# Gathered table rows of a PEER layer: groups of 16 u rows and 16 v rows turned into single u and v rows, the v rows 22 behind

## Chip, core and metric

The kernel runs on one core of a Trainium2 chip. The metric is the device time of one execution in microseconds (us). TensorE (PE in the profile), VectorE (DVE), ScalarE (ACT), GpSimd (POOL) and SyncE (SP) each work through an instruction stream of their own, in order. SP starts most of the DMA transfers, POOL starts the gathers.

## What is computed

One layer of a streaming encoder: a convolution and a differential-attention head group, then a PEER layer, each with a residual and a layer norm. There are 544 tokens of width 1024: 512 of a prompt and 32 of running streams. The change lies in the PEER layer. For every token and each of 8 heads it picks 16 of 16384 rows of a table `u_tab` by product keys (two times 128 half scores, the best 16 of each, the best 16 of their sums), and then computes:

```python
a = jnp.einsum('td,thkd->thk', tb, u_tab[e]).astype(jnp.float32)
a = jax.nn.gelu(a, approximate=False) * g
return jnp.einsum('thk,thkd->td', a.astype(tb.dtype), v_tab[e])
```

`e` holds the 128 (8 heads of 16) row numbers of a token, and `g` their softmax weights.

## The kernel before

**Dense part.** For the first 384 tokens (three tiles of 128, `TA = 3`) the kernel multiplies with the whole tables. `u_part(j)`, called for j = 0 to 127, takes one block of 128 u rows: `split` loads it (`raw`, 512 KB, line 898, on SP's queue), ACT makes a rounded copy `hi` (L900), DVE the rest `lo = raw - hi` (L902), and PE runs 24 matmuls of 128x384 into one PSUM tile `pat` (L911): 8 with `hi`, 8 with `lo`, 8 with `hi` again (against the low half of the tokens). ACT puts the Gelu of `pat` into `ge` (L917). `v_part` and `v_mm` do the same with 128 blocks of v rows, 18 matmuls of 128x512 per block (L994).

**Gathered part.** The last 160 tokens do not go through the dense part. They stand in two tiles: one of 128 tokens, and one of 32 tokens in 4 copies, each copy with 32 of the 128 row numbers. So there are 128 + 32 = 160 *columns*, and for each column one gather of a u row and one of a v row: an indirect DMA on POOL (L847) that fetches 128 rows of 4 KB, one for each partition, into a buffer `rowg`, of which there are four. For a u row, DVE multiplies it with the tokens and sums up (L858, the *dot*, into one column of `aB`). For a v row, DVE adds it, times a weight of each partition, to the sum `accB` (L869, the *add*; the first is L867). The weights of 16 columns are the Gelu of 16 columns of `aB` (L861, ACT) times `GW` (L862, DVE). The generator `b_gather` emits this, one gather and its dot or add at each step: 320 steps in all, in groups of 16 u rows, Gelu, 16 v rows.

**What sets the order.** `gathers(rate)` takes some steps of the generator; `slot()` calls it after each `u_part` and each v block, and `query()` after each of its key blocks `hp` from the third on. `slot()` also emits pieces of the *background*, the choice of rows for the dense tokens (`level2`: top-16 searches, L661 to L666, and arithmetic, L721 to L773, on DVE) and their one-hot matrices (`onehots`: L810 to L817 on DVE, L826 on PE). Each gather is *paced*: it gets a dependence on a matmul, `ANCHOR[-1 - LAG]` with `LAG = 2`; the first matmul of each `u_part` is put on the list `ANCHOR`, so a gather that is emitted behind a `u_part` waits for the first matmul of the `u_part` two calls earlier. Behind all this stands a scheduler, which reorders the instructions of every engine by its own model of their times before the program is built; so the order in the source is only its input.

Of the kernel before, what the change touches and what calls it, by code (L numbers as in the profile page):

```python
# [8 lines left out]
F32 = mybir.dt.float32  # L9
F32R = mybir.dt.float32r  # L10
F16 = mybir.dt.float16
I32 = mybir.dt.int32
U32 = mybir.dt.uint32
AF = mybir.ActivationFunctionType
OP = mybir.AluOpType
# [4 lines left out]
D = 1024  # L20
# [7 lines left out]
TA = NA // 128  # L28
# [32 lines left out]
EXTRA = 8  # L61
RUN = 4
LAST = 4
CN = (3, -1)
CB = 4
CZ = 2
# [10 lines left out]
def build(tc, I, O):  # L77
# [3 lines left out]
    V, S, G, PE, SY = nc.vector, nc.scalar, nc.gpsimd, nc.tensor, nc.sync  # L81
# [165 lines left out]
    for c in range(4):  # L247
# [5 lines left out]
        for d0, h, s0, s1 in ((30, 0, 0, HT), (30 + HT, 1, 0, np2), (572, 1, np2, HT)):  # L253
            V.scalar_tensor_tensor(U[:, c, d0:d0 + s1 - s0], p0[:, h, s0:s1], bzc[:, c:c + 1], sg[:, h, s0:s1],
                                   op0=OP.add, op1=OP.mult)
# [26 lines left out]
    def conv(n):  # L282
        for _ in range(n):
            next(taps, None)
# [18 lines left out]
    for m in range(2):  # L303
        V.scalar_tensor_tensor(lj, lamv[:, 2 * m], 1.0, lamv[:, 2 * m + 1], op0=OP.mult, op1=OP.mult,
                               accum_out=lsum[:, m:m + 1])
# [123 lines left out]
    for h in range(4):  # L429
        qk = [None, None]  # L430
        for kind in (1, 0):
            n = 8 + 4 * kind + h
# [18 lines left out]
        qh, kh = qk  # L451
        if (h, -1) == CN:
            conv(124)
# [3 lines left out]
        for i in ((0, 1, 2, 3) if h < 3 else (3, 0, 1, 2)):  # L457
# [17 lines left out]
            conv(CB)  # L475
            if (h, i) == CN:
                conv(124)
# [45 lines left out]
    tk = pool(ctx, "tk", 1)  # L523
    idxB = [tk.tile([128, 128], I32, name="idx0"), tk.tile([128, 32], I32, name="idx1")]
    GWB = [tk.tile([128, 128 if i < 4 else 32], F32, name=f"GW{i}") for i in (3, 4)]
    aB = [tk.tile([128, 128], F32, name="aB0"), tk.tile([128, 32], F32, name="aB1")]
    VT, IT, IJ, GW = {}, {}, {}, {}
# [20 lines left out]
    for s in range(2):  # L548
        t = op_.tile([128, D], F32, tag="row", name="bg", bufs=4) if s == 0 else xhB[0]
# [123 lines left out]
    def run(g):  # L673
        for _ in g:
            pass
# [156 lines left out]
    accB = [gap.tile([128, D], F32, name=f"accB{s}") for s in range(2)]  # L832
    gp = pool(ctx, "gp", 1, side="right")
# [5 lines left out]
    h2B = xhB  # L839
# [5 lines left out]
    def gather(tab, idx):  # L845
        t = gp.tile([128, D], F32, tag="rowg", name="rowg", bufs=ROWB)
        g = G.indirect_dma_start(out=t, out_offset=None, in_=tab, in_offset=bass.IndirectOffsetOnAxis(ap=idx, axis=0))  # L847
        if len(ANCHOR) > LAG:
            tc.add_manual_dep(g.ins, ANCHOR[-1 - LAG].ins.name, DEP, reason="paced by the dense tiles")
        return t  # L850

    def b_gather():
        for s, n in ((0, 128), (1, 32)):
            for c0 in range(0, n, 16):
                for q in range(c0, c0 + 16):
                    t = gather(I["u_ji"], idxB[s][:, q:q + 1])
                    jk = gp.tile([128, D], F16, tag="jkg", name="jkg", bufs=1)
                    V.scalar_tensor_tensor(jk, t, 1.0, h2B[s], op0=OP.mult, op1=OP.mult, accum_out=aB[s][:, q:q + 1])  # L858
                    yield
                w = tk.tile([128, 16], F32, tag="wB", name="wB", bufs=2)  # L860
                S.activation(w, aB[s][:, c0:c0 + 16], AF.Gelu)  # L861
                V.tensor_mul(w, w, GW[TA + s][:, c0:c0 + 16])  # L862
                for q in range(c0, c0 + 16):
                    t = gather(I["vd"], idxB[s][:, q:q + 1])
                    ac = accB[s]
                    if q == 0:
                        V.tensor_scalar(ac, t, w[:, 0:1], None, op0=OP.mult)  # L867
                    else:
                        V.scalar_tensor_tensor(ac, t, w[:, q - c0:q - c0 + 1], ac, op0=OP.mult, op1=OP.add)  # L869
                    yield  # L870

    state = {"A": 0, "gdone": 0, "budget": 0.0, "gq": 0.0, "slots": 2 * NK}

    def gathers(rate):
# [7 lines left out]
        return n  # L882

    gat = b_gather()
    query(h2fA, (0, 1, 2), NA)
    q1.close()
# [4 lines left out]
    h2B = xhB  # L891
# [72 lines left out]
    def v_part(j):  # L964
        if j % JC == 0:
            GC[0] = gcp.tile([128, NBLK, JC, GB], F32, tag="gc", name="gc")
            SY.dma_start(GC[0].rearrange("p b j t -> p b (j t)"),
                         g_d[:, :, j:j + JC, :].rearrange("b i j t -> i b (j t)"))
        ge = GE.pop(j)
        if ge is None:  # L970
            ge = gcp.tile([128, NA], F32, tag="gel", name="gel", bufs=3)
            SY.dma_start(ge, ge_d[j])  # L972
        early = NK - LAST <= j < NK - 2
        pp, tags = (dn, ("ge",) * 3) if early else (vpp, ("P", "Ph", "Pl"))
        nb = ND if early else 2
        P = pp.tile([128, NA], F32, tag=tags[0], name="P", bufs=nb).rearrange("p (b t) -> p b t", t=GB)
        V.tensor_mul(P, ge.rearrange("p (b t) -> p b t", t=GB), GC[0][:, :, j % JC, :])
        Ph = pp.tile([128, NA], F32R, tag=tags[1], name="Ph", bufs=nb)
        Pf = P.rearrange("p b t -> p (b t)")
        S.copy(Ph, Pf)  # L980
        Pl = pp.tile([128, NA], F32R, tag=tags[2], name="Pl", bufs=nb)
        V.tensor_sub(Pl, Pf, Ph.bitcast(F32))  # L982
        vp_ = (uvp, RAWB, HIB) if early else (vpp, VRAWB, VHIB)
        vh, vl = split(I["vd"][j * 128:(j + 1) * 128, :], *vp_)
        return Ph, Pl, vh, vl

    def v_mm(j, tiles, parts):
        Ph, Pl, vh, vl = parts
        for i in tiles:
            sl = slice(i * 128, (i + 1) * 128)  # L990
            for hf in range(2):
                hs = slice(hf * 512, (hf + 1) * 512)
                for n, (a, b) in enumerate(((Ph, vh), (Pl, vh), (Ph, vl))):
                    mm = PE.matmul(accs[i][hf], a[:, sl], b[:, hs], start=(j == 0 and n == 0), stop=(j == NK - 1 and n == 2))  # L994
                    if i == hf == n == 0:
                        ANCHOR.append(mm)

    for j in range(NK - LAST):
        v_mm(j, range(TA), v_part(j))
# [5 lines left out]
    run(gat)  # L1005
    vs = {j: v_part(j) for j in range(NK - LAST, NK)}
    for i in range(TA):
# [135 lines left out]
```

## Time and profile before

| | |
|---|---|
| Time, median of 3 runs | 1684.15 us (1680.67 to 1685.24) |
| Profiled execution: time, and its span | 1685.61 us, 1683.8 us |
| Mean granted TensorE clock (1 is full) | 0.975 |
| PE busy | 1612.9 us (96%) |
| DVE busy | 1391.9 us (83%) |
| ACT busy | 623.9 us (37%) |
| POOL busy | 436.6 us (26%) |

The busy shares are averages over the whole span. The gathers run from 442 to 1641 us of the span: the query and the background lie at 442 to about 840, the u blocks alone and then u and v blocks in turn behind that, and the tail begins at about 1645.

### The profile page before, as it was taken

How to read it: one execution, taken by the hardware profiler on the slowest of the kernel's cores; microseconds unless marked ns; L12 is line 12 of the kernel's file. 1: busy time of each engine (PE TensorE's matmuls, PEld its weight loads, DVE VectorE, ACT ScalarE, POOL GpSimd, SP SyncE). 2: the span in 40 equal slices, each digit the busy share in tenths (PEclk: the TensorE clock that was granted, in tenths of full speed). 3: DMA queues.
4: the chain of work that ended last, by engine and by line, in shares of the span. 5: the costliest groups of instructions: out<-in, count | busy, mean ns of one | idle time of the engine just before them, and what ended most of it. 6: DMA issues, size and time to landing. Idle time of an engine off the chain costs nothing.

```text
span 1683.8 us, 24735 instructions
## 1 busy us (share of the span) xinstructions
PE 1612.9 (96%) x8911; PEld 1399.1 (83%) x8911; DVE 1391.9 (83%) x2674; ACT 623.9 (37%) x1073; POOL 436.6 (26%) x325
## 2 busy tenths in 40 slices
PE   7999987999979999999999999999999999999996
PEld 4878855786669999999899889888888888888885
DVE  3878988799899999898688567888777778788897
ACT  3312566342114443444344333333333333333333
POOL 0000000000245343133322213443334234335540
PEclk8999978999989999999999999999999999999998
DMA  9766243363578889898888998999999999999993
GB/s 351 272 216 222 73 139 116 103 222 113 199 217 303 283 277 314 289 322 271 305 283 315 344 348 323 334 355 353 324 351 341 336 332 349 328 324 330 344 319 119
DMA packets 184538, 465.59 MB, mean 277 GB/s; under 512 B 17536, under 2 KB 85184, under 8 KB 181216
## 3 DMA queue, kind: packets, MB, share of 16 engines
q1 hardware_dynamic: 138336, 296.23, 51.1%
q0 software_dynamic: 46080, 167.79, 28.9%
q8 instruction: 70, 1.15, 0.3%
q14 instruction: 52, 0.43, 0.1%
HBM read 415.57 MB, written 45.77 MB: 274 GB/s over the span
## 4 chain that ended last, share of the span: by engine, by line
PE 82%; DVE 7%; DMA 5%; ACT 2%; issue 2%; SPq 2%; POOL 0%; DVEq 0%; ACTq 0%
PE acc L994 30%; PE pat L911 30%; PE big L826 5%; PE big L191 3%; PE pat L191 2%; PE big L582 2%; PE pat L685 2%; PE pat L152 1%; PE pat L316 1%; DMA raw<-in_uT_dram 1%; DMA rowg<-in_u_ji_dram,idx 1%; DVE s L664 1%; SPq L972 1%; DMA rt<-mod_d 1%; DVE IT L662 1%
## 5 line engine op out<-in xcount | busy, mean ns | idle before, releaser
L847 POOL DMA_INDIRECT rowg<-in_u_ji_dram,idx x160 | 202.5, 1265 | 825.8 <-DVE VT L661 443.9
L902 DVE TENSOR_TENSOR lo<-raw,hi 128x1024 fp32r<-128x1024 f32 x256 | 312.0, 1220 | 119.9 <-ACT hi L900 117.5
L900 ACT CAST hi<-raw 128x1024 fp32r<-128x1024 f32 x256 | 266.7, 1046 | 311.3 <-PE acc L994 217.0
L847 POOL DMA_INDIRECT rowg<-in_vd_dram,idx x160 | 232.7, 1455 | 371.0 <-DVE accB L869 89.1
L994 PE MATMUL acc<-hi,Pl 128*128 128x512 f32 x768 | 300.1, 391 | 0.0
L994 PE MATMUL acc<-lo,Ph 128*128 128x512 f32 x768 | 281.3, 390 | 0.0
L994 PE MATMUL acc<-hi,Ph 128*128 128x512 f32 x768 | 244.2, 392 | 2.4 <-issue 2.4
L911 PE MATMUL pat<-h2h,hi 128*128 128x384 f32 x1024 | 214.7, 345 | 6.9 <-ACT hi L900 3.8
L911 PE MATMUL pat<-h2h,lo 128*128 128x384 f32 x1024 | 211.5, 343 | 4.3 <-DVE lo L902 4.3
L911 PE MATMUL pat<-h2l,hi 128*128 128x384 f32 x1024 | 210.4, 341 | 0.0
L869 DVE SCALAR_TENSOR_TENSOR accB<-rowg,wB,accB 128x1024 f32<-128x1024 f32 x158 | 201.8, 1278 | 3.7 <-DMA rowg<-in_vd_dram,idx 3.3
L858 DVE SCALAR_TENSOR_TENSOR jkg<-rowg,xhB 128x1024 f16<-128x1024 f32 x160 | 194.8, 1217 | 9.5 <-DMA rowg<-in_u_ji_dram,idx 7.4
L911 PEld LDWEIGHTS pat<-h2h,hi 128*128 128x128 f32 x1024 | 183.8, 191 | 14.1 <-ACT hi L900 6.2
L911 PEld LDWEIGHTS pat<-h2h,lo 128*128 128x128 f32 x1024 | 184.1, 190 | 7.7 <-DVE lo L902 4.6
L911 PEld LDWEIGHTS pat<-h2l,hi 128*128 128x128 f32 x1024 | 184.5, 190 | 2.6
L994 PEld LDWEIGHTS acc<-hi,Ph 128*128 128x128 f32 x768 | 143.7, 188 | 29.8 <-issue 2.9
L994 PEld LDWEIGHTS acc<-lo,Ph 128*128 128x128 f32 x768 | 144.2, 188 | 29.1
L994 PEld LDWEIGHTS acc<-hi,Pl 128*128 128x128 f32 x768 | 144.1, 188 | 28.0
L917 ACT ACTIVATE ge<-pat 128x384 f32<-128x384 f32 x128 | 62.6, 490 | 197.5 <-PE pat L911 151.1
L980 ACT CAST Ph<-P 128x384 fp32r<-128x384 f32 x128 | 65.1, 511 | 140.6 <-issue 89.7
L826 PE MATMUL big<-Yg,X 128*128 128x128 f16 x768 | 99.9, 297 | 0.0
L982 DVE TENSOR_TENSOR Pl<-P,Ph 128x384 fp32r<-128x384 f32 x128 | 70.6, 553 | 33.9 <-ACT Ph L980 32.3
(303 smaller groups left out, 1973.3 us busy)
## 6 DMA issues: line engine op xcount, KB each, us to landing
raw<-in_uT_dram SPq DMA_DIRECT2D x128, 512.0 KB
raw<-in_vd_dram SPq DMA_DIRECT2D x128, 512.0 KB
wr<-in_w_ada_dram SPq DMA_DIRECT2D x48, 512.0 KB
g_d<-stg SPq DMA_DIRECT2D x24, 1024.0 KB
gc<-g_d SPq DMA_DIRECT2D x16, 1536.0 KB
wq<-in_w_query_dram SPq DMA_DIRECT2D x32, 512.0 KB
ge_d<-ge SPq DMA_DIRECT2D x70, 192.0 KB
gel<-ge_d SPq DMA_DIRECT2D x70, 192.0 KB
```

Source lines behind the costliest of these rows:

```text
L191: PE.matmul(p[h], a[:, k * 128:(k + 1) * 128], b[:, k, h * HT:(h + 1) * HT], start=(q == 0 and k == 0), stop=(q == 2 and k == KC - 1))
L826: PE.matmul(pg[:, t, :], X[:, u, :, r], Yg[:, n, u, :, r], start=(n == 0), stop=(n == 1))
L847: g = G.indirect_dma_start(out=t, out_offset=None, in_=tab, in_offset=bass.IndirectOffsetOnAxis(ap=idx, axis=0))
L858: V.scalar_tensor_tensor(jk, t, 1.0, h2B[s], op0=OP.mult, op1=OP.mult, accum_out=aB[s][:, q:q + 1])
L869: V.scalar_tensor_tensor(ac, t, w[:, q - c0:q - c0 + 1], ac, op0=OP.mult, op1=OP.add)
L900: S.copy(hi, raw)
L902: V.tensor_sub(lo, raw, hi.bitcast(F32))
L911: mm = PE.matmul(p[:, :NA], a[:, k * 128:(k + 1) * 128], b[:, k, :], start=(n == 0), stop=(n == 23))
L917: S.activation(ge, p[:, :NA], AF.Gelu)
L980: S.copy(Ph, Pf)
L982: V.tensor_sub(Pl, Pf, Ph.bitcast(F32))
L994: mm = PE.matmul(accs[i][hf], a[:, sl], b[:, hs], start=(j == 0 and n == 0), stop=(j == NK - 1 and n == 2))
```

## The change

`b_gather` becomes a pipeline of single rows. At each of its rounds it emits one u row (gather and dot) and, 22 rounds later (`GLAG = 22`), the v row of that column (gather and add). So it begins with 23 u rows, then one v row and one u row take turns, and it ends with 22 v rows. The weights are still made for 16 columns at once, now when the first v row of the 16 is due. The number of steps (320), of gathers, dots, adds, Gelus and multiplies stays.

```diff
--- before.py
+++ after.py
@@ -61,6 +61,7 @@
 EXTRA = 8
 RUN = 4
 LAST = 4
+GLAG = 22
 CN = (3, -1)
 CB = 4
 CZ = 2
@@ -850,24 +851,38 @@
         return t
 
     def b_gather():
-        for s, n in ((0, 128), (1, 32)):
-            for c0 in range(0, n, 16):
-                for q in range(c0, c0 + 16):
-                    t = gather(I["u_ji"], idxB[s][:, q:q + 1])
-                    jk = gp.tile([128, D], F16, tag="jkg", name="jkg", bufs=1)
-                    V.scalar_tensor_tensor(jk, t, 1.0, h2B[s], op0=OP.mult, op1=OP.mult, accum_out=aB[s][:, q:q + 1])
-                    yield
-                w = tk.tile([128, 16], F32, tag="wB", name="wB", bufs=2)
-                S.activation(w, aB[s][:, c0:c0 + 16], AF.Gelu)
-                V.tensor_mul(w, w, GW[TA + s][:, c0:c0 + 16])
-                for q in range(c0, c0 + 16):
-                    t = gather(I["vd"], idxB[s][:, q:q + 1])
-                    ac = accB[s]
-                    if q == 0:
-                        V.tensor_scalar(ac, t, w[:, 0:1], None, op0=OP.mult)
-                    else:
-                        V.scalar_tensor_tensor(ac, t, w[:, q - c0:q - c0 + 1], ac, op0=OP.mult, op1=OP.add)
-                    yield
+        cols_ = [(s, q) for s, n in ((0, 128), (1, 32)) for q in range(n)]
+        wb = {}
+
+        def dot(s, q):
+            t = gather(I["u_ji"], idxB[s][:, q:q + 1])
+            jk = gp.tile([128, D], F16, tag="jkg", name="jkg", bufs=1)
+            V.scalar_tensor_tensor(jk, t, 1.0, h2B[s], op0=OP.mult, op1=OP.mult, accum_out=aB[s][:, q:q + 1])
+
+        def weights(s, c0):
+            w = tk.tile([128, 16], F32, tag="wB", name="wB", bufs=2)
+            S.activation(w, aB[s][:, c0:c0 + 16], AF.Gelu)
+            V.tensor_mul(w, w, GW[TA + s][:, c0:c0 + 16])
+            wb[s] = w
+
+        def add(s, q):
+            t = gather(I["vd"], idxB[s][:, q:q + 1])
+            ac, w = accB[s], wb[s]
+            if q == 0:
+                V.tensor_scalar(ac, t, w[:, 0:1], None, op0=OP.mult)
+            else:
+                V.scalar_tensor_tensor(ac, t, w[:, q % 16:q % 16 + 1], ac, op0=OP.mult, op1=OP.add)
+
+        for n in range(len(cols_) + GLAG):
+            if n < len(cols_):
+                dot(*cols_[n])
+                yield
+            if n >= GLAG:
+                s, q = cols_[n - GLAG]
+                if q % 16 == 0:
+                    weights(s, q)
+                add(s, q)
+                yield
 
     state = {"A": 0, "gdone": 0, "budget": 0.0, "gq": 0.0, "slots": 2 * NK}
```

Lines move by 1 from L64 on and by 15 behind the generator: the gather is L848 after, the dot L860, the add L874, `lo` L917, the u matmuls L926.

The scheduler's order changes on every engine. The first place is POOL, whose rows are almost nothing but gathers. The number behind a name is that of the buffer as it is allocated in the source, so it also tells what was emitted ahead of what. Before, at the 14th to 21st gather (`in_u_ji` are u rows, `in_vd` v rows):

```order
L847 DMA rowg_4579<-in_u_ji_dram,idx0_2933 128x1024
L847 DMA rowg_4620<-in_u_ji_dram,idx0_2933 128x1024
L847 DMA rowg_4624<-in_u_ji_dram,idx0_2933 128x1024
L847 DMA rowg_4668<-in_vd_dram,idx0_2933 128x1024
L847 DMA rowg_4671<-in_vd_dram,idx0_2933 128x1024
L847 DMA rowg_4711<-in_vd_dram,idx0_2933 128x1024
L847 DMA rowg_4751<-in_vd_dram,idx0_2933 128x1024
L847 DMA rowg_4754<-in_vd_dram,idx0_2933 128x1024
```

The same place after, and the rows that follow it:

```order
L848 DMA rowg_4579<-in_u_ji_dram,idx0_2933 128x1024
L848 DMA rowg_4620<-in_u_ji_dram,idx0_2933 128x1024
L848 DMA rowg_4624<-in_u_ji_dram,idx0_2933 128x1024
```

```order
L848 DMA rowg_4796<-in_u_ji_dram,idx0_2933 128x1024
L848 DMA rowg_4800<-in_u_ji_dram,idx0_2933 128x1024
L848 DMA rowg_4844<-in_vd_dram,idx0_2933 128x1024
L848 DMA rowg_4847<-in_u_ji_dram,idx0_2933 128x1024
L848 DMA rowg_4895<-in_vd_dram,idx0_2933 128x1024
L848 DMA rowg_4957<-in_u_ji_dram,idx0_2933 128x1024
L848 DMA rowg_5018<-in_vd_dram,idx0_2933 128x1024
L848 DMA rowg_5066<-in_u_ji_dram,idx0_2933 128x1024
L848 DMA rowg_5070<-in_vd_dram,idx0_2933 128x1024
```

Before, v rows follow on the 16th u row at once; after, u rows go on up to the 23rd, and v and u rows take turns from there.

The second place is DVE between the eighth and the ninth `lo` (`lo_5208` and `lo_5245` before, `lo_5219` and `lo_5255` after). Before:

```order
L902 TENSOR_TENSOR lo_5208<-raw_5204,hi_5206 128x1024
L665 MAX v2_4902<-s2_4912 128x8
L665 MAX v2_4902<-s2_4954 128x8
L869 SCALAR_TENSOR_TENSOR accB0_4134<-rowg_5009,wB_4665,accB0_4134 128x1024
L666 MAX_INDEX x2_4903<-v2_4902,s2_4906 128x8
L666 MAX_INDEX x2_4903<-v2_4902,s2_4912 128x8
L666 MAX_INDEX x2_4903<-v2_4902,s2_4954 128x8
L902 TENSOR_TENSOR lo_5245<-raw_5241,hi_5243 128x1024
```

After (the last 12 rows up to the tenth `lo`; between `lo_5219` and these stand one dot, a cast and eight MAX):

```order
L860 SCALAR_TENSOR_TENSOR jkg_5198,aB0_2937<-rowg_5196,xhB0_2920 128x1024
L725 TENSOR_TENSOR dl_4900<-f_4898 128x240
L663 MAX_INDEX x2_4911<-v2_4910,cd_4902 128x8
L665 MATCH_REPLACE s2_4914<-v2_4910,cd_4902 128x50
L663 MAX_INDEX x2_4911<-v2_4910,cd_4902 128x8
L665 MATCH_REPLACE s2_4920<-v2_4910,cd_4902 128x50
L663 MAX_INDEX x2_4911<-v2_4910,cd_4902 128x8
L665 MATCH_REPLACE s2_4963<-v2_4910,cd_4902 128x50
L663 MAX_INDEX x2_4911<-v2_4910,cd_4902 128x8 x5
L874 SCALAR_TENSOR_TENSOR accB0_4134<-rowg_5248,wB_4841,accB0_4134 128x1024
L917 TENSOR_TENSOR lo_5255<-raw_5251,hi_5253 128x1024
L917 TENSOR_TENSOR lo_5309<-raw_5305,hi_5307 128x1024
```

Two more adds and two more dots of gathered rows now stand ahead of the ninth `lo`, in this stretch, and the tenth follows directly. From the end of the 16th dot, which is the same instruction in both, up to the ninth `lo` there are 18 gathered rows' operations after (12 dots, 6 adds) and 12 before (12 adds).

The third place is DVE up to the 17th `lo` (`lo_5704` before, `lo_5709` after). Before:

```order
L858 SCALAR_TENSOR_TENSOR jkg_5452,aB0_2937<-rowg_5450,xhB0_2920 128x1024
L752 TENSOR_TENSOR pr_5066<-pr_5066 128x896
L666 MAX_INDEX x2_6433<-v2_6432,s2_6436 128x8
L666 MAX_INDEX x2_6433<-v2_6432,s2_6442 128x8
L666 MAX_INDEX x2_6433<-v2_6432,s2_6448 128x8
L902 TENSOR_TENSOR lo_5625<-raw_5621,hi_5623 128x1024
L858 SCALAR_TENSOR_TENSOR jkg_5494,aB0_2937<-rowg_5492,xhB0_2920 128x1024
L752 TENSOR_TENSOR pr_5066<-pr_5066 128x512
L664 MATCH_REPLACE s2_6454<-v2_6432,cd_6387 128x50
L664 MATCH_REPLACE s2_6500<-v2_6432,cd_6387 128x50
L664 MATCH_REPLACE s2_6506<-v2_6432,cd_6387 128x50
L902 TENSOR_TENSOR lo_5704<-raw_5700,hi_5702 128x1024
```

After:

```order
L874 SCALAR_TENSOR_TENSOR accB0_4134<-rowg_5660,wB_4841,accB0_4134 128x1024
L917 TENSOR_TENSOR lo_5631<-raw_5627,hi_5629 128x1024
L860 SCALAR_TENSOR_TENSOR jkg_5740,aB0_2937<-rowg_5738,xhB0_2920 128x1024
L753 TENSOR_TENSOR pr_5076<-pr_5076 128x896
L667 MAX_INDEX x2_6442<-v2_6441,s2_6445 128x8
L667 MAX_INDEX x2_6442<-v2_6441,s2_6451 128x8
L667 MAX_INDEX x2_6442<-v2_6441,s2_6457 128x8
L874 SCALAR_TENSOR_TENSOR accB0_4134<-rowg_5780,wB_4841,accB0_4134 128x1024
L917 TENSOR_TENSOR lo_5709<-raw_5705,hi_5707 128x1024
```

Two adds have come in (`accB0`), and three MATCH_REPLACE and one L752 stand behind the `lo` now. From the end of the 16th dot up to this `lo` there are 18 dots and 12 adds after, 8 dots and 16 adds before. The last gathered row ahead of this `lo` is `rowg_5780`. By its number it was emitted behind the `u_part` of `lo_5751`, so its anchor is the first matmul with `hi_5629`. PE's order after, from that matmul up to the matmuls that need the 17th `lo`:

```order
L926 MATMUL pat_5633<-h2h_2918,hi_5629 128x384 x8
L926 MATMUL pat_5593<-h2h_2918,lo_5591 128x384 x8
L926 MATMUL pat_5593<-h2l_2919,hi_5589 128x384 x8
L926 MATMUL pat_5711<-h2h_2918,hi_5707 128x384 x8
L926 MATMUL pat_5633<-h2h_2918,lo_5631 128x384 x8
L926 MATMUL pat_5633<-h2l_2919,hi_5629 128x384 x8
L926 MATMUL pat_5711<-h2h_2918,lo_5709 128x384 x8
```

In the order before, the row with the same place in the emission, `rowg_5775`, is used (by a dot) ahead of the 21st `lo`, `lo_5911`, and on PE 16 groups of 8 matmuls, the anchor's among them, stand ahead of the group that needs that `lo`; after, it is 6 groups.

## Rows read from the trace of the kernel before

**Rows 1.** Page: the chain that ended last, by engine.

```profile
PE 82%; DVE 7%; DMA 5%; ACT 2%; issue 2%; SPq 2%; POOL 0%; DVEq 0%; ACTq 0%
```

**Rows 2.** Waits of PE from 440 us: engine, line, releaser, us in all, times, longest.

```profile
PE sm L691 <- ACT q L687: 5.6, 1, 5.6
PE pat L911 <- DVE lo L902: 4.3, 1, 4.3
PE pat L911 <- ACT hi L900: 3.8, 1, 3.8
PE pat L911 <- ACT ge L917: 2.6, 2, 1.5
PE acc L994 <- issue: 2.4, 1, 2.4
```

**Rows 3.** Windows: stretch and length, busy of PE, PEld, DVE, ACT, POOL, PE clock, DMA share, GB/s.

```profile
500.00:540.00 40.00, 40.00 (x217) 40.00 (x217) 38.20 (x126) 12.88 (x19) 19.56 (x14) 0.95 0.85 287
540.00:580.00 40.00, 39.89 (x227) 39.48 (x226) 40.00 (x140) 18.58 (x24) 15.62 (x13) 1.00 0.86 294
580.00:620.00 40.00, 39.68 (x223) 38.68 (x222) 39.28 (x95) 16.77 (x26) 17.68 (x12) 1.00 0.82 279
720.00:830.00 110.00, 109.89 (x708) 106.39 (x706) 92.60 (x100) 45.05 (x72) 36.41 (x23) 1.00 0.88 297
1000.00:1600.00 600.00, 600.00 (x2826) 520.57 (x2825) 481.65 (x627) 211.64 (x296) 235.75 (x174) 1.00 0.97 337
```

**Rows 4.** Timeline, PE then ACT, the stalls at 485 and 499: start, us, [idle before <- releaser].

```profile
485.05 1.65 PE L691 MATMUL sm<-skT,q 128*128 128x128 f32 x6 [5.62 <-ACT q L687]
...
499.28 2.93 PE L911 MATMUL pat<-h2h,lo 128*128 128x384 f32 x8 [4.27 <-DVE lo L902]
...
484.42 0.21 ACT L861 ACTIVATE wB<-aB 128x16 f32<-128x16 f32 x1 [12.35 <-DVE jkg L858]
```

**Rows 5.** Page: the dot and the add of gathered rows on DVE.

```profile
L869 DVE SCALAR_TENSOR_TENSOR accB<-rowg,wB,accB 128x1024 f32<-128x1024 f32 x158 | 201.8, 1278 | 3.7 <-DMA rowg<-in_vd_dram,idx 3.3
L858 DVE SCALAR_TENSOR_TENSOR jkg<-rowg,xhB 128x1024 f16<-128x1024 f32 x160 | 194.8, 1217 | 9.5 <-DMA rowg<-in_u_ji_dram,idx 7.4
```

**Rows 6.** Timeline, DVE then PE, around the 17th `lo` (558.74).

```profile
556.72 1.22 DVE L858 SCALAR_TENSOR_TENSOR jkg<-rowg,xhB 128x1024 f16<-128x1024 f32 x1
...
557.86 0.42 DVE L752 TENSOR_TENSOR pr<-pr 128x512 f16<-128x512 f16 x1
...
558.74 1.22 DVE L902 TENSOR_TENSOR lo<-raw,hi 128x1024 fp32r<-128x1024 f32 x1
...
561.30 1.57 PE L911 MATMUL pat<-h2h,lo 128*128 128x384 f32 x8
562.71 1.57 PE L911 MATMUL pat<-h2l,hi 128*128 128x384 f32 x8
```

**Rows 7.** Timeline, DVE then PE, around the ninth `lo`.

```profile
523.11 1.21 DVE L902 TENSOR_TENSOR lo<-raw,hi 128x1024 fp32r<-128x1024 f32 x1
...
527.01 1.57 PE L911 MATMUL pat<-h2h,lo 128*128 128x384 f32 x8
```

**Rows 8.** Timeline, POOL then DVE: one gather and its dot.

```profile
526.27 1.78 POOL L847 DMA_INDIRECT rowg<-in_u_ji_dram,idx  x1 [1.15 <-DVE s L664]
...
531.51 1.23 DVE L858 SCALAR_TENSOR_TENSOR jkg<-rowg,xhB 128x1024 f16<-128x1024 f32 x1 [1.05 <-DMA rowg<-in_u_ji_dram,idx]
```

**Rows 9.** Chain, 440 to 505 us: start, us, what.

```profile
451.04 8.49 DMA rowg<-in_u_ji_dram,idx
```

**Rows 10.** Gathers of v rows, 490 to 640 us: duration on POOL min/median/max in ns.

```profile
L847 POOL DMA_INDIRECT rowg<-in_vd_dram,idx x27: 936/1654/3661, 490.8 to 628.9; - x27
```

**Rows 11.** Chain, 800 to 840 us.

```profile
822.64 10.19 DMA raw<-in_uT_dram
```

**Rows 12.** Timeline, PE, after the stall at 830.

```profile
834.00 2.93 PE L911 MATMUL pat<-h2h,hi 128*128 128x384 f32 x8 [3.79 <-ACT hi L900]
836.73 2.45 PE L911 MATMUL pat<-h2h,lo 128*128 128x384 f32 x8
```

## The prediction

> **What bounds the kernel now.** I read the chain of work that ended last first: 82% of it is PE, 7% DVE, 5% DMA [rows 1]. So the kernel is a row of PE work with a few holes, and the question is which holes the change opens or closes. PE's waits from 440 us on, where the gathers begin, name all of them: 5.6 us once for the query (L691), 4.3 us once for `lo`, 3.8 us once for `hi`, 2.6 us for `ge` and 2.4 us before a v matmul [rows 2], 18.7 us together. The windows show how near the next holes are. From 500 to 620 us PE is busy 119.57 of 120 us, but DVE too, 117.48 of 120; from 720 to 830 PE is full still, and DVE has 17 of 110 us free; from 1000 to 1600 PE is busy in all 600 us and DVE in 482 [rows 3]. So for some 120 us behind the query two engines are at their limit together. DVE work that comes earlier there must hold up PE, as soon as a `lo` is late; behind 720 it need not. What PE loses early isn't won back, since PE has no free time in 1000 to 1600 us.
>
> **The first two holes stay.** At 485.05 PE had waited 5.62 us for a copy on ACT, which stood behind the first Gelu of 16 columns; that Gelu had waited 12.35 us for DVE's 16th dot, to 484.42 [rows 4]. This looks like the very thing that a pipeline removes. But the orders of PE, DVE, ACT and POOL are the same in both programs up to this dot and this Gelu: the Gelu, though emitted 6 rows later, is put at the same place and still stops ACT's queue. The 4.27 us at 499.28 [rows 4] wait for the third `lo`, ahead of which stand 5 gathered rows' operations in both. I count no gain for either.
>
> **What moves on DVE.** No work is added or removed: 160 dots, 160 adds, 10 Gelus stay, and a dot costs 1.217 us and an add 1.278 [rows 5]. But u rows can go on while no weight is ready, and the scheduler uses it to put gathered rows earlier, ahead of other DVE work and of `lo`. Up to the 17th `lo` there are 10 more dots and 4 fewer adds, and 3 MATCH_REPLACE and one L752 fewer. The dots cost 10 x 1.217 = 12.2 us, or 11.4 where I take the 1.14 from a dot's start to the next instruction's (556.72 to 557.86) [rows 6]. The adds give back 4 x 1.278 = 5.1 [rows 5]. The L752 and the three MATCH_REPLACE took 0.9 together, from 557.86 to the start of `lo` at 558.74 [rows 6]. So this `lo` comes 12.2 - 5.1 - 0.9 = 6.2 us later at most, 5.4 at least; I take 5.8.
>
> What cover is there? Before, this `lo` ran from 558.74 for 1.22 us, so it was there at 559.96, and PE came to it at 561.30 [rows 6]: 1.3 us of slack. PE's order for these groups gives no more: no group has been put ahead of the ones that wait. So PE stalls by 5.8 - 1.3 = **4.5 us** by this point (4.1 to 4.9). This is the sum of all holes up to there, not one hole. A part falls at the ninth `lo`: 12 more dots and 6 fewer adds ahead of it make 12 x 1.217 - 6 x 1.278 = 6.9 us, less some small DVE operations. It was there at 524.32 and needed at 527.01 [rows 7], 2.7 us of slack, and PE's order now has one group more ahead of it, 1.4 us (a group of 8 matmuls each 1.41 us: 561.30 to 562.71 [rows 6]). That leaves at most 6.9 - 2.7 - 1.4 = 2.8 us, a first piece of the 4.5. Behind 620 us the order after is ahead by 3 to 7 gathered rows, but there DVE has free time to pay with, so I add nothing.
>
> **What moves on POOL.** The anchors don't move: each gather, by its place in the emission, waits for the same matmul. Its use moves. `rowg_5780` is used ahead of the 17th `lo`, 6 groups of PE after its anchor, 6 x 1.41 = 8.5 us; before, the row of the same place had 16 groups, 22.6 us. The trip of one gather is in the rows: POOL starts at 526.27, and DVE, which was waiting, starts the dot at 531.51: 5.2 us [rows 8]. Another transfer took 8.49 us [rows 9]. Behind it stand the add (1.28) and `lo` (1.22) [rows 5, 6]: 5.2 + 1.3 + 1.2 = 7.7 us against 8.5 is just in time, 8.49 + 1.3 + 1.2 = 11.0 is 2.5 us late. This is a wait that DVE hardly has before (7.4 and 3.3 us in all) [rows 5]. Counted in the same way, 14 of the 40th to 60th gather have a lead of 8.5 to 10.1 us. Some four of them can follow one upon the other as a loop, in which DVE waits for POOL, POOL for PE and PE for DVE; each turn costs 0 to 2.5 us, so the term is 0 to 10. The shorter trip is the one seen in this stretch, the longer one was a transfer ahead of it, so I take a value near the lower end: **2 us**.
>
> The Trainium skill has a fit for such a transfer ("DMA: Bandwidth & Descriptors", "Anatomy of one DMA — SWDGE (gpsimd) path"): a fixed 2.0 us plus the bytes at 436 GB/s. For 512 KB that makes an estimate of 3.2 us, and the sum without this term; the trace has 5.2 and 8.49 us [rows 8, 9], and I go by the trace.
>
> **PE's clock.** After the 3.79 us hole at 834.00 the next two groups of 8 took 2.93 and 2.45 us [rows 12], where one takes 1.57 [rows 6]: 2.2 us more. After the 4.27 us hole the first took 2.93 too [rows 4]. The holes that I expect are pieces of 1 to 3 us, so I add nothing; the bound is 2.2 us for each that gets as long as 3.8.
>
> **At nothing.** ACT, the tail and the v blocks: the last add is done well ahead of PE's last matmuls in both orders, and from 1000 us DVE has 118 of 600 us free [rows 3], which hides any other order there. If this cover failed, a late `lo` would cost what it is late, an operation's 1.2 us at a time.
>
> **Sum.** 4.5 + 2 = 6.5 us on the profiled execution's 1685.6 gives 1692.1. That execution lay 1.5 us above the median of 1684.15, so against the median: 1690.7, +0.4%. Without any loop the sum is 1688.7.
>
> **The rivals.** A measurement can hardly tell 0.3% (5 us) from no change, so "no change" is 1679 to 1689.
> - *The stall is absorbed.* Here the holes fall at places with more cover than the 17th `lo` has, as the ninth with 2.7 us and a group put ahead, and gathers come in time: PE loses 0 to 4 us, 1684 to 1688. It decides if the new order is late by less than about 4 us where the slack is least. For it speaks that every piece beside the 17th `lo` has more cover; against it that DVE was busy 40.00 of 40 us in 540 to 580 [rows 3], so that nothing between could take up a delay.
> - *Faster: the late holes close.* The `hi` hole of 3.79 us follows a 512 KB load of u rows that took 10.19 us [rows 11]; with its 2.2 us of clock it costs 6.0, and `ge` (2.6) and the v matmul (2.4) [rows 2] make it 11.0. By then the gathers stand several rows ahead, and another meeting of transfers on the DMA engines may let this load come in time. All of it together gives 1684.2 + 6.5 - 11.0 = 1679.7; faster by over 0.3% needs these holes closed and less than about 6 us lost early. For it speaks that the first of these holes rests on one slow load; against it that the anchors, which set when gathers start, stay.
> - *Much slower: POOL is late.* From 490 to 640 us the gathers of v rows held POOL 0.94 to 3.66 us, 1.65 in the middle [rows 10]. At the upper end a trip is 5.2 + 3.66 - 1.78 = 7.1 us, and with add and `lo` 9.6, late by 1.1; with transfers of 8.49 us it is 2.5 each. Four loops at 2.5, and two holes long enough for the clock, make 4.5 + 10 + 4.4 = 19 us: 1703. The Trainium skill ("SBUF — State Buffer", the note on the "DVE blocks DMA" trap) says that descriptors written on GpSimd can be held up while VectorE holds the port pair that both share. The spread of POOL's times agrees with that and doesn't show it, since DVE ran nearly all the time.
> - *It does nothing*, because the scheduler restores the old order, is excluded: the orders differ.
>
> **How the numbers follow.** My forecast, +4.5 to +12 us, has 0.46; absorbed 0.30; late holes closed 0.14, of which most ends near no change or below; POOL late 0.10. The predicted time is 1690.7. The range reaches from the faster rival's end, 1679, to most of the POOL rival, 1702; the forecast's own range is 1688 to 1696. Slower by over 0.3% takes most of the forecast (0.43) and POOL late (0.10), so 0.53; faster 0.12; the same 0.35.
>
> **What would show it.** Right: PE's waits at the `lo` line (L917 after) rise from 4.3 to about 9 to 11 us in pieces of 1 to 3 us between 515 and 620 us, PE's busy time of 119.57 of 120 us in 500 to 620 falls by about 5, DVE's waits for `rowg` grow beyond 10.7 us, and the 5.62 us at 485 are there as before. Wrong: if the hole at 485 is gone or shorter; if PE is as full as before in 500 to 620; if the holes of `hi`, `ge` and the v matmul [rows 2] are gone; or if new holes stand behind 700 us, where I count none.

## The result, and the profile after

The changed kernel took 1694.04 us (median of 6 runs, 1690.96 to 1695.39), the kernel before 1682.92 (6 runs, 1679.64 to 1685.24): 11.1 us slower, a ratio of 1.0065 (95% interval 1.0049 to 1.0081). The profiled execution after took 1693.14 us, 0.9 less than its median, and that of before 1685.61, 2.7 more than its median. So between the two traces (spans of 1691.4 and 1683.8 us) there are only 7.6 of the 11.1 us. The likeliest time in the prediction was 1690.7.

PE's waits from 440 us on, to be read against [rows 2]:

```profile
PE pat L926 <- DVE lo L917: 12.4, 8, 5.4
PE sm L692 <- ACT q L688: 4.7, 1, 4.7
PE pat L926 <- ACT hi L915: 4.3, 6, 1.5
PE big L827 <- DVE X L818: 2.0, 1, 2.0
PE acc L1009 <- issue: 1.8, 1, 1.8
```

In place of one wait for `lo` (4.3 us) there are eight (12.4 us); the longest, 5.4, is the one near 499 us that was there before. The one long wait for `hi` (3.8 us) has gone; the six that stand there now are short. The wait for the query's copy, which the change might have removed, is there as before. DVE's own waits say why `lo` is late. Here are the two groups that wait for gathered rows; on the page of before they were 3.3 and 7.4 us [rows 5]:

```profile
DVE accB L874 <- DMA rowg<-in_vd_dram,idx: 34.2, 18, 4.1
...
DVE jkg L860 <- DMA rowg<-in_u_ji_dram,idx: 17.4, 15, 4.4
```

DVE now stands 51.6 us for rows that are still under way, 33 times (10.7 us and 8 times before). The windows show where it hurts PE (the first number behind the length is PE's busy time, the third DVE's):

```profile
500.00:620.00 120.00, 111.98 (x603) 107.44 (x603) 108.24 (x350) 43.10 (x60) 48.57 (x36) 0.98 0.77 258
620.00:720.00 100.00, 96.73 (x615) 92.47 (x615) 85.38 (x100) 41.90 (x66) 29.01 (x20) 1.00 0.86 298
720.00:830.00 110.00, 107.53 (x685) 103.28 (x684) 94.85 (x107) 45.30 (x72) 29.01 (x21) 0.98 0.86 294
830.00:1000.00 170.00, 166.42 (x1019) 159.13 (x1018) 121.22 (x129) 66.24 (x105) 41.07 (x34) 1.00 0.91 315
```

For the first and third of these, before had 119.57 and 109.89 of PE [rows 3]. For the other two:

```profile
620.00:720.00 100.00, 100.00 (x647) 97.06 (x646) 87.59 (x106) 41.84 (x64) 31.70 (x21) 1.00 0.87 300
...
830.00:1000.00 170.00, 161.26 (x961) 152.49 (x960) 122.65 (x132) 68.03 (x105) 36.30 (x31) 0.98 0.92 321
```

From 500 to 830 us PE is busy 13.2 us less than before (7.6, 3.3 and 2.4). DVE was at its limit before, 117.48 of 120 us [rows 3]; now it works 108.24 and is idle for the rest, though PE waits for it. So DVE isn't overloaded: it waits. From 830 to 1000 us PE gets 5.2 us back. The chain of work through 500 to 640 us shows the trips themselves (start, us, what):

```profile
514.87 7.24 DMA rowg<-in_u_ji_dram,idx
...
527.88 8.85 DMA rowg<-in_vd_dram,idx
...
537.99 6.87 DMA rowg<-in_u_ji_dram,idx
...
563.24 5.17 DMA rowg<-in_u_ji_dram,idx
...
583.54 7.22 DMA rowg<-in_vd_dram,idx
...
607.82 7.04 DMA rowg<-in_vd_dram,idx
```

Six trips of 5.2 to 8.9 us, 42.4 us of 140, lie on the chain, where before there was PE work. A trip also stands ahead of the 2.0 us that PE waits for `X` (L818), at 723 us:

```profile
709.93 10.63 DMA rowg<-in_vd_dram,idx
```

One turn of the loop in full, on POOL, PE, and DVE (start, us, idle before and what ended it):

```profile
527.88 2.32 POOL L848 DMA_INDIRECT rowg<-in_vd_dram,idx  x1 [2.41 <-DMA rowg<-in_u_ji_dram,idx]
...
535.59 3.36 PE L926 MATMUL pat<-h2h,hi 128*128 128x384 f32 x16
...
536.20 0.94 POOL L848 DMA_INDIRECT rowg<-in_vd_dram,idx  x1 [3.32 <-PE pat L926]
536.84 1.28 DVE L874 SCALAR_TENSOR_TENSOR accB<-rowg,wB,accB 128x1024 f32<-128x1024 f32 x1 [3.07 <-DMA rowg<-in_vd_dram,idx]
...
538.22 1.22 DVE L917 TENSOR_TENSOR lo<-raw,hi 128x1024 fp32r<-128x1024 f32 x1
...
539.49 1.68 PE L926 MATMUL pat<-h2h,lo 128*128 128x384 f32 x8 [0.54 <-DVE lo L917]
```

The gather starts at 527.88; DVE needs its row at 533.8 and stands 3.07 us, until 536.84; the `lo` behind it comes at 538.22, where without the wait it would come at 535.15, and PE, busy up to 538.95 with two groups that the scheduler had put ahead, waits another 0.54 us for it.

### The profile page after: what moved, and what is told of

It reads as the page before. It is cut to its first block, busy times and chain, and to the rows that moved or that the text cites. A ratio compares the mean times of both kernels' runs of the same rounds, so it can differ in the third digit from the quotient of the medians.

```text
span 1691.4 us, 24599 instructions
## 1 busy us (share of the span) xinstructions
PE 1616.3 (96%) x8911; PEld 1395.9 (83%) x8911; DVE 1389.5 (82%) x2674; ACT 622.6 (37%) x1073; POOL 414.4 (25%) x325
## 4 chain that ended last, share of the span: by engine, by line
PE 73%; DVE 11%; DMA 8%; issue 5%; ACT 2%; POOL 1%; SPq 1%; DVEq 0%; POOLq 0%; ACTq 0%
PE acc L1009 30%; PE pat L926 22%; PE big L827 4%; PE big L192 3%; DMA rowg<-in_vd_dram,idx 2%; PE pat L192 2%; PE pat L686 2%; PE big L583 2%; DMA rowg<-in_u_ji_dram,idx 2%; DVE jkg L860 2%; PE pat L153 1%; DMA ge_d<-ge 1%; DVE s L665 1%; PE pat L317 1%; DVE lo L917 1%
## 5 line engine op out<-in xcount | busy, mean ns | idle before, releaser
L917 DVE TENSOR_TENSOR lo<-raw,hi 128x1024 fp32r<-128x1024 f32 x256 | 311.5, 1221 | 110.1 <-ACT hi L915 104.5
L848 POOL DMA_INDIRECT rowg<-in_u_ji_dram,idx x160 | 199.7, 1248 | 805.1 <-DVE VT L662 441.3
L848 POOL DMA_INDIRECT rowg<-in_vd_dram,idx x160 | 213.3, 1333 | 417.8 <-PE pat L926 170.8
L874 DVE SCALAR_TENSOR_TENSOR accB<-rowg,wB,accB 128x1024 f32<-128x1024 f32 x158 | 201.9, 1278 | 34.3 <-DMA rowg<-in_vd_dram,idx 34.2
L926 PE MATMUL pat<-h2h,lo 128*128 128x384 f32 x1024 | 215.2, 346 | 12.5 <-DVE lo L917 12.4
L926 PE MATMUL pat<-h2h,hi 128*128 128x384 f32 x1024 | 212.9, 342 | 6.0 <-ACT hi L915 4.3
L860 DVE SCALAR_TENSOR_TENSOR jkg<-rowg,xhB 128x1024 f16<-128x1024 f32 x160 | 194.6, 1217 | 20.1 <-DMA rowg<-in_u_ji_dram,idx 17.4
L926 PE MATMUL pat<-h2l,hi 128*128 128x384 f32 x1024 | 209.9, 342 | 0.0
L926 PEld LDWEIGHTS pat<-h2h,lo 128*128 128x128 f32 x1024 | 183.8, 191 | 20.0 <-DVE lo L917 16.2
L926 PEld LDWEIGHTS pat<-h2h,hi 128*128 128x128 f32 x1024 | 181.7, 189 | 15.9 <-ACT hi L915 7.7
L926 PEld LDWEIGHTS pat<-h2l,hi 128*128 128x128 f32 x1024 | 185.5, 190 | 2.2
L1009 PEld LDWEIGHTS acc<-hi,Ph 128*128 128x128 f32 x768 | 143.6, 188 | 29.2 <-issue 2.5
L274 DVE SCALAR_TENSOR_TENSOR acc<-U,wdw,acc 128x574 f32<-128x574 f32 x120 | 96.5, 804 | 1.4
```

Of the source, the lines that this page charges most:

```text
L274: t = V.scalar_tensor_tensor(acc[:, c], U[:, c, w:w + CO], wdw[:, c, w:w + 1], acc[:, c], op0=OP.mult, op1=OP.add)
L874: V.scalar_tensor_tensor(ac, t, w[:, q % 16:q % 16 + 1], ac, op0=OP.mult, op1=OP.add)
L917: V.tensor_sub(lo, raw, hi.bitcast(F32))
L926: mm = PE.matmul(p[:, :NA], a[:, k * 128:(k + 1) * 128], b[:, k, :], start=(n == 0), stop=(n == 23))
```

## The experiments

Two theories stood at the start. *Lead* is the PE work between a gather's anchor and the first use of its row. **Trip**: the new order uses a row before its transfer can be there. **Order**: too many dots and adds stand ahead of `lo`, so that DVE's work itself makes it late. Times are medians, each with its ratio to the kernel before on the same chip.

**1. A longer lead (use_lead4, use_lead2).** Each dot, and each add but the first of a tile, gets a dependence on the first matmul of the u block emitted last, which keeps the scheduler from putting it close behind its gather; use_lead4 also has `LAG = 4`.

```diff
+    def late_use(op):
+        if len(ANCHOR) > LAG:
+            tc.add_manual_dep(op.ins, ANCHOR[-1].ins.name, DEP, reason="paced by the dense tiles")
...
-            V.scalar_tensor_tensor(jk, t, 1.0, h2B[s], ...)
+            late_use(V.scalar_tensor_tensor(jk, t, 1.0, h2B[s], ...))
...
-                V.scalar_tensor_tensor(ac, t, w[:, q % 16:q % 16 + 1], ac, ...)
+                late_use(V.scalar_tensor_tensor(ac, t, w[:, q % 16:q % 16 + 1], ac, ...))
```

> The changed kernel with two dependences altered: each gather is released two u blocks earlier (LAG 4 in place of 2), and each dot and add also waits for the first matmul of the u block emitted last, so that the scheduler can't put it close behind its gather. In the built order no gathered row is used less than 16.6 us of PE work after its anchor among the 33rd to 64th (8.5 in the changed kernel), while about as many gathered rows stand ahead of the ninth u block's lo (34 in both; 28 in the kernel before) and of the 17th (44; 46; 40). Theory 'trip' (DVE stands waiting for rows that are still under way): DVE's waits for rowg fall from 51.6 us to under 15, and at least 5 us of the 11 lost come back: 1682 to 1689. Theory 'order' (too many dots and adds ahead of lo): the waits may fall, but PE's waits for lo stay near 12 us and the time at 1691 to 1696.

> As use_lead4, but with the gathers released where they were (LAG 2): the shortest lead of the 33rd to 64th row goes from 8.5 to 10.4 us only, rows ahead of the 17th lo 44. 'Trip': trips of 5.2 us in time, those of 8.5 us still late by about a microsecond, so DVE waits 20 to 40 us for rowg and the time lies between, 1687 to 1693. 'Order': the same as use_lead4 to within 2 us, 1691 to 1696.

Measured: use_lead4 1682.27 us, 0.9997 (0.9986 to 1.0009); use_lead2 1686.06 us, 1.0016 (1.0003 to 1.0029). With later use of the same rows the whole loss is gone in the first, and most of it in the second. DVE's waits for rows and PE's windows in use_lead4:

```profile
DVE accB L878 <- DMA rowg<-in_vd_dram,idx: 5.8, 10, 1.0
...
DVE jkg L864 <- DMA rowg<-in_u_ji_dram,idx: 2.9, 4, 1.3
```

```profile
500.00:620.00 120.00, 115.13 (x635) 112.18 (x634) 116.47 (x361) 46.90 (x66) 59.48 (x37) 0.99 0.81 278
620.00:720.00 100.00, 99.75 (x648) 95.99 (x647) 88.97 (x106) 43.55 (x70) 34.15 (x22) 1.00 0.88 308
720.00:830.00 110.00, 109.85 (x706) 105.98 (x705) 90.42 (x100) 44.86 (x70) 34.41 (x22) 1.00 0.87 302
830.00:1000.00 170.00, 166.76 (x1000) 158.65 (x999) 124.90 (x132) 68.76 (x105) 51.90 (x33) 1.00 0.93 325
```

The waits are 8.7 us. Of the 13.2 us that PE lost from 500 to 830 us, 8.5 have come back (324.73 against 316.24), and DVE works 116.47 of 120 us again. That is the trip's share in these windows. 4.7 us are still lost against before (329.46), most of it in one hole, ahead of the ninth `lo`:

```profile
528.82 1.99 PE L930 MATMUL pat<-h2h,lo 128*128 128x384 f32 x8 [3.35 <-DVE lo L921]
```

In use_lead2 DVE waited 7.6 us, far under the 20 to 40 expected: a shortest lead of 10.4 us, 1.9 more than in the changed kernel, was enough for nearly all trips. From 500 to 830 us its PE is busy 326.19 us, 3.3 less than before; the earlier release of use_lead4 gave nothing there. What it has over use_lead4 lies outside that stretch, above all a hole of 4.9 us ahead of a v matmul near 972 us.

That trips didn't become longer can be read from the kernel before itself. The trace behind [rows 8] has no landing times, but that of its second execution (before_again, below) has them. For the 44 gathers from 490 to 640 us:

```profile
DMA to landing us min/median/max: 4.3/6.2/10.4
```

The trace of the changed kernel has no landing times either, but in its variants the middle is 6.1 (lag4_only, below), 6.0 (use_lead2) and 6.5 us (use_lead4). So what the change shortened is the lead; the trip is as long without it.

**2. Earlier release alone (lag4_only).** `LAG = 4` in the changed kernel, nothing else.

> The changed kernel with LAG 4 alone: gathers are released two u blocks (8.5 us) earlier, but the scheduler, by its own times, puts dots and adds earlier too (47 rows ahead of the 17th lo, 46 in the changed kernel), so that the shortest leads stay at 8.5 us (10 rows under 10.2). 'Trip': DVE's waits for rowg stay high, 25 to 55 us, and the time at 1688 to 1695; so it is the lead in the order, not the release as such, that counts. Rival 'release' (gathers simply start too late in the changed kernel): waits fall under 15 us and the time to 1681 to 1686, as in use_lead4, which altered both.

Measured: 1697.83 us, 1.0095 (1.0079 to 1.0111). It is no help, it is slower still. DVE waits 29.2 us for rows:

```profile
DVE accB L874 <- DMA rowg<-in_vd_dram,idx: 18.7, 17, 3.0
DVE jkg L860 <- DMA rowg<-in_u_ji_dram,idx: 10.5, 11, 2.4
```

The waits are in the expected band and the rival falls: the scheduler uses the earlier release to place the dots and adds earlier as well. DVE waits 22 us less than in the changed kernel, but PE is as idle from 500 to 830 us (busy 315.57 us, and 316.24). The waits alone don't set PE's loss, then; the order may have a part, with 4 more rows ahead of the 29th `lo` (63, 59), which no run shows by itself. The median is above the expected band, and the trace can't say why: the profiled execution, at 1693.06 us, is the fastest of six that reach to 1704.34.

**3. A lighter order with short leads, and the control (after_q1, before_q1).** `QG = 1.0` in both kernels: fewer rows are emitted during the query.

> The changed kernel with fewer gathered rows emitted during the query (QG 1.0 in place of 1.8): only 24 and 34 rows stand ahead of the ninth and the 17th lo (34 and 46 in the changed kernel, 28 and 40 in the kernel before), but the leads are as short as in the changed kernel (8.5 us at the shortest, 19 of the 17th to 64th row under 10.2). 'Order': with 6 rows fewer than before ahead of the 17th lo, PE waits less for lo than before, and the time is at 1675 to 1684. 'Trip': DVE waits for rowg as long as in the changed kernel, 35 us or more, and the time stays at 1689 to 1696.

> Control: the kernel before with QG 1.0. 22 rows ahead of the seventh lo, 33 ahead of the 17th, leads mostly 25 us but 11 of the 17th to 64th under 10.4. 'Order': faster than before by what DVE had too much up to 620 us, 1677 to 1682. 'Trip': a few waits more than the kernel before, 15 to 25 us, and a time of 1682 to 1687.

Measured: after_q1 1707.78 us, 1.0143 (1.0121 to 1.0164); before_q1 1699.29 us, 1.0094 (1.0076 to 1.0112). Both missed every band, because the gathers that were put off ended late: the last add, at 1640.81 before, came at 1659 us in before_q1 and 1675 us in after_q1, and the tail behind the start of PE's last v matmul grew from 15.6 us to 29.5 and 32.8. So these runs are read up to that matmul alone. It starts at 1668.25 in the kernel before and 1678.47 in the changed one; with `QG = 1.0`, before and changed:

```profile
1666.61 0.40 PE L994 MATMUL acc<-lo,Ph 128*128 128x512 f32 x1
```

```profile
1677.85 0.40 PE L1009 MATMUL acc<-lo,Ph 128*128 128x512 f32 x1
```

The executions don't start level, though: the first group of u matmuls with `lo` starts at 477.33 us before and 474.71 after, and with `QG = 1.0` at 474.94 and 477.19. From there to the last v matmul the change costs 12.8 us, and 9.0 with `QG = 1.0`, where 34 rows stand ahead of the 17th `lo` in place of 46. A second execution of the kernel before is 2.6 us shorter in this measure, so neither number is better than that. The 9.0 speak for the trip (DVE waited 54.1 us in after_q1, 20.4 in before_q1), and against the order as the larger part.

**4. Short leads in the kernel before (before_q14), and a lighter order with long leads (use_lead4_q14, use_lead4_q16, use_lead4_q14_g16).** `QG = 1.4` or 1.6; in the last, `GLAG = 16` too.

> The kernel before with QG 1.4. Up to the 17th lo its order is as heavy as before (28 and 39 rows ahead of the ninth and the 17th; 28 and 40), but its leads are short now: 9.5 us at the shortest and 14 in the middle for the 33rd to 64th row (22.6 and 26.8). 'Trip': DVE's waits for rowg rise from 11 to 20 to 40 us, PE loses 2 to 6 us more in 500 to 720 us, and the time is 1685 to 1690. 'Order' alone: no change, 1681 to 1685.

Measured: 1702.14 us, 1.0107 (1.0088 to 1.0126). Here the order is as heavy as before and only the leads are short. DVE's waits for rows and PE's window:

```profile
DVE jkg L858 <- DMA rowg<-in_u_ji_dram,idx: 12.8, 8, 3.1
...
DVE accB L869 <- DMA rowg<-in_vd_dram,idx: 6.1, 8, 1.3
```

```profile
500.00:620.00 120.00, 114.29 (x621) 110.69 (x620) 111.14 (x345) 45.72 (x64) 50.59 (x32) 0.97 0.76 249
```

18.9 us of waits (the lowest end of the band is missed by one), and PE is busy 5.3 us less than before in 500 to 620 us: short leads alone, without the change, bring such a loss (2.0 of it, at 612 us, is a wait for `hi` and not for `lo`). The time is far above the band for another reason, the tail (below).

> use_lead4 with QG 1.4 in place of 1.8: the leads stay long (18.7 us at the shortest for the 33rd to 64th row), and only the order becomes lighter: 29 rows ahead of the ninth lo (34 in use_lead4) and 38 ahead of the 17th (44; 40 in the kernel before). 'Order' as the second part of the loss: the 4.9 us that PE loses in 500 to 620 us in use_lead4 fall under 1.5, and the time to 1677 to 1680, faster than both kernels. Rival 'tail': the rows left for later push the last adds behind PE's end, as with QG 1.0, and the time is 1683 or more.

> As use_lead4_q14 with QG 1.6: 32 rows ahead of the ninth lo, 41 ahead of the 17th. 'Order': PE loses 1 to 3 us in 500 to 620 us, and the time lies between the two, 1678 to 1682. If the order is no cost at all once the leads are long, the three do not differ by more than 1.5 us.

> use_lead4_q14 with the v rows 16 behind in place of 22: the same order up to the 200th lo but for u and v rows changed in turn, and 6 v rows fewer at the very end. If the distance itself is worth nothing, the same as use_lead4_q14 to within 2 us; if the end of the last v rows is what limits there, 2 to 5 us faster.

Measured: use_lead4_q14 1696.88 us, 1.0074 (1.0060 to 1.0089); use_lead4_q16 1681.95 us, 0.9990 (0.9980 to 1.0000); use_lead4_q14_g16 1696.85 us, 1.0077 (1.0062 to 1.0092). The windows of the first bear the order out:

```profile
500.00:620.00 120.00, 119.17 (x669) 116.32 (x668) 117.85 (x364) 49.23 (x70) 52.95 (x34) 0.99 0.79 262
...
830.00:1000.00 170.00, 161.28 (x964) 152.92 (x963) 117.26 (x125) 64.41 (x97) 50.76 (x33) 0.98 0.90 310
```

With 29 rows ahead of the ninth `lo` in place of 34, PE's idle time in 500 to 620 us goes from 4.9 to 0.8 us; in use_lead4_q16, with 32 rows, it is 1.2. That is 4.0 us for the order, with the leads long in all three. But the time is not 1677: PE gives 5.5 us back in 830 to 1000 (161.28, and 166.76 in use_lead4), and the tail is almost 17 us longer. The chain of its end, and of use_lead4_q16:

```profile
1639.86 28.34 PE acc L1013 x125
1668.20 1.73 PE pat L1073 x4
```

```profile
1645.68 1.72 PE pat L1073 x4
1647.39 22.50 PE acc L1013 x99
```

The four matmuls of L1073 (L1054 before), which wait for the last add of the second gathered tile, stand in the midst of the last v matmuls in the second and behind all of them in the first. So the output of those 32 tokens, and what stands behind it in DVE's order, begins only then, and the span ends 29.1 us after the v matmuls (1668.20 to 1697.3) in place of 12.5 (1670.56 to 1683.1). The scheduler picked that order; the last add itself came 3.6 us later (1646.32, and 1642.76). `GLAG` changes nothing here (0.03 us). So both theories' terms are there, and the rival on the tail came true with them. before_q14 has the same long tail (29.5 us), with the four matmuls behind the last v matmul too.

**5. The distance (glag48).** `GLAG = 48` in the changed kernel.

> The changed kernel with the v rows 48 behind. Up to the 20th lo its order has nearly as many gathered rows ahead as the kernel before (41 ahead of the 17th; 40 and 46), with leads of 20 us in the middle; then v rows join, and the leads go to 12 to 18 us, 5 of the 33rd to 64th under 10.2. 'Trip': waits of DVE for rowg between 15 and 35 us, most of them behind 590 us, and a time of 1685 to 1691. 'Order': the stall of 500 to 590 us is gone but comes later, where DVE has time to spare: 1680 to 1685.

Measured: 1690.96 us, 1.0038 (1.0024 to 1.0052), at the upper edge of the trip's band. DVE waited 37.2 us, a little above the band, and PE is busy less than before by 4.3 us in 500 to 620 us, 2.3 in 620 to 720 and 1.9 in 720 to 830, with all its holes but the known one at 496 from 590 us on, where the v rows join. A hole of 6.1 us ahead of a v matmul at 983 us (2.4 in the kernel before) is in the time too, so it is the places of the holes that speak for the trip and not the time.

**6. The hole at 485 us (use_lead4_gelu).** The Gelu is wrapped in `late_use` too.

> use_lead4, in which the Gelu of the weights also waits for the first matmul of the u block emitted last. In the built order the first Gelu now stands on ACT behind the last copy of the query (it stood ahead of it). If the hole of 5.5 us at 485 us is due to that Gelu alone, it is gone, and the time is 4 to 6 us under use_lead4's: 1676.5 to 1678.5. Rival: PE's loss moves to the next hole, the wait for the third lo, which DVE makes at the same time as before: that wait grows from 5.1 to about 10 us, and the time stays at 1681 to 1684.

Measured: 1691.66 us, 1.0045 (1.0032 to 1.0057). The hole at 485 is gone, and the next one takes it over whole, as the rival had it:

```profile
498.73 2.93 PE L930 MATMUL pat<-h2h,lo 128*128 128x384 f32 x8 [10.80 <-DVE lo L921]
```

10.8 us in place of 5.5 and 5.1: DVE is what limits up to the third `lo`, and the Gelu on ACT only decides where PE stands. That the time is 9 us above use_lead4's isn't explained by this; 3.6 us of it lie behind 830 us (163.14 of 170 us busy, and 166.76), and the rest is open.

**7. The kernel before once more (before_again).**

> The kernel before, profiled once more. Open: whether the hole of 3.8 us at 834 us, ahead of which a 512 KB load of u rows took 10.2 us, and the 2.4 us ahead of a v matmul belong to the kernel or to that one execution. If to the kernel, holes of 6 us and more stand between 800 and 1000 us again; if to the execution, they lie elsewhere or are gone. The two holes at 485 and 499 us, and waits of DVE for rowg of about 11 us, should come again.

Measured: 1682.28 us in one run. The hole of `hi` is there again, 3.90 us, with the same slow group behind it:

```profile
831.62 2.93 PE L911 MATMUL pat<-h2h,hi 128*128 128x384 f32 x8 [3.90 <-ACT hi L900]
```

So it belongs to the kernel, as do the holes of `ge` (2.6 us) and ahead of the v matmul (2.2). DVE's waits for rows were 6.8 us, where about 11 were expected. That the changed kernel doesn't have the hole of `hi` is an effect of its order, but not of the change in particular: before_q14 and before_q1, without the change, don't have it there either.

## Why the prediction was right, and where its sum was off

*The holes that stay.* Right. The two at 485 and 499 us came again, as 4.73 and 5.37 us after and 4.16 and 5.19 in before_again; together they are about 10 us each time, and in experiment 6 closing the first only made the second longer.

*DVE's order, 4.5 us.* Right in mechanism and size: use_lead4, whose leads are long, still lost 4.7 us from 500 to 830 us, and 4.0 of it went with a lighter order in use_lead4_q14. Its longest piece, 3.35 us at the ninth `lo`, is near the 2.8 "at most".

*POOL's trip, 2 us.* This is the term that was mis-sized: 8.5 us, inside its bounds of 0 to 10 but near the upper one. I took the 5.2 us of one gather for the trip and the 8.49 us as one that stood behind another transfer. But 6.2 us are the middle in the kernel before (before_again, experiment 1), and 6.2 + 1.3 + 1.2 = 8.7 us already miss a lead of 8.5. The six trips on the chain after took 5.2 to 8.9, four of them about 7. So such a lead is missed by many trips and not by a few. The Trainium skill's fit ("DMA: Bandwidth & Descriptors", "Anatomy of one DMA — SWDGE (gpsimd) path") gave an estimate of 3.2 us for such a transfer. The traces don't agree: 4.3 us is the shortest of the 44 trips, with the DMA engines busy 0.84 of the time from 500 to 620 us.

*Nothing behind 620 us.* Wrong: 5.6 us of the 13.2 were lost from 620 to 830, 2.0 of them at 723, behind the trip of 10.63 us. In use_lead4 the loss there is 0.3. Free time of DVE as a share does not help against a row that isn't there; it only helps against more work.

*The clock, at nothing.* Right in the net, but not as it was reasoned, from long holes alone. Behind the hole of 2.1 us at 526 the granted clock of 526 to 531 us was 0.79, and of 720 to 740, with the 2.0 us hole, 0.91; before, both were 1.00. On the other side the slow stretch behind the `hi` hole is gone: 830 to 840 us had 0.66 before and 1.00 after.

*The late holes.* I gave their closing a chance of 0.14 and left it out of the sum. The one of `hi` did close, with the change and in use_lead4 alike, and PE gained 5.2 us from 830 to 1000. What closed it isn't shown; use_lead4_q14 and use_lead4_q16, without that hole, have another, of 7.2 and 7.4 us, ahead of the first v matmul.

*The tail, at nothing.* It became shorter by 2.7 us: from the start of PE's last v matmul (1668.25 and 1678.47) to the end of the span it took 15.6 before and 12.9 after. The cause isn't shown.

The profiled span by these terms: 4.7 + 8.5 - 5.2 - 2.7 = 5.3, where 7.6 was measured. Two things are missing in it. The executions didn't start level: the first u matmuls with `lo` start 2.6 us earlier after, though the orders of the engines don't differ up to there. And from there to the last v matmul the same matmuls, holes left out, took 1177.1 us after and 1172.3 before, 4.8 more, a cost that the prediction had at nothing. With both, 5.3 + 4.8 - 2.6 = 7.5. In use_lead4 they are gone (1172.2); but the second execution of the kernel before has 1170.1, so about 2 us can be no more than the spread of executions. What makes them is open: a group behind a hole takes longer (2.48 us behind the 2.12 us hole at 528, 1.57 without one), but the mean granted clock of the span is no lower (0.983, and 0.975 before).

So the forecast lay closer than its terms by luck: the trip and the slower matmuls cost more than was thought, and the `hi` hole and the tail gave back what was not counted. Two of the prediction's own signs of being wrong came true, the `hi` hole that closed and new holes behind 700 us.

**Of the rivals,** "absorbed" and "POOL is late" were decided by the trip: the second was the nearer one in mechanism, as trips of about 7 us on the chain set PE's holes, but POOL itself was no slower: from 490 to 640 us the gathers of v rows held it 1.2 us in the middle after, and 1.65 before [rows 10]. No version came out clear ahead of the kernel before. use_lead4_q16 is nearest, at 0.9990 with an interval that reaches 1.0000, which is within what I called no change.

## What to carry to other kernels

A finer pipeline can remove the backlog that hid a transfer. Before, the row that was looked at in the prediction was used 16 groups of matmuls behind its anchor, which hid its trip; with single rows the scheduler used it 6 groups behind. (It is not the grouping alone that keeps the lead long: before_q14 has groups and short leads. That the scheduler's own times for a gather are shorter than the chip's is likely, but not shown.) Look, in the order that is built, at how much work lies between a transfer's release and the first engine that needs its result, and compare it with the trips of the trace at their upper end; where it is short, a dependence that delays the use can be worth more than an earlier release. And ask of an engine that is idle 10% in a stretch whether it has spare time or is waiting.

## What was not expected of the chip

Two holes of the same length cost PE different amounts. After, on PE:

```profile
528.31 2.48 PE L926 MATMUL pat<-h2h,lo 128*128 128x384 f32 x8 [2.12 <-DVE lo L917]
```

```profile
595.47 1.68 PE L926 MATMUL pat<-h2h,lo 128*128 128x384 f32 x8 [2.12 <-DVE lo L917]
```

Both holes are 2.12 us long. Behind the first, a group of 8 took 2.48 us, behind the second 1.68, where one without a hole takes 1.57 [rows 6]. The granted clock (1 is 2.4 GHz, and the other level 1.2) was 1.00 in 510 to 526 us, ahead of the first hole, and 0.79 in 526 to 531; in 590 to 600 us, around the second, it stayed at 1.00. So a hole's length alone didn't tell whether the clock fell after it.
